# One pair of gate/up units per SwiGLU by block products in place of two, weight loads in written order, the third sum on VectorE, and the SiLU as one ScalarE function

## The chip, the cores and the metric

The kernel runs on one core of a Trainium2 chip, as one program in one launch. The metric is the device time in microseconds from start to end; three runs of the kernel before were timed, and one execution was profiled.

The engines are named as the profile names them: PE is TensorE (its weight loads are shown apart as PEld), DVE is VectorE, ACT is ScalarE, POOL is GpSimd, SP is SyncE, which only issues transfers here. L12 is line 12 of the kernel.

## The reference

Four layers over 256 tokens of width 1024, all in float32. Each layer is: half a SwiGLU, a token mixer beside a cross-attention into 256 memory tokens, and half a SwiGLU again.

```
h = rms_norm(x, ffn_norm[i, 0]);  x = x + 0.5 * swiglu(h, w_gate, w_up, w_down)
h = rms_norm(x, mix_norm[i]);     x = x + concat(mixer(h), memory_attention(h)) @ w_out[i]
h = rms_norm(x, ffn_norm[i, 1]);  x = x + 0.5 * swiglu(h, ...)

swiglu(x, wg, wu, wd) = (silu(x @ wg) * (x @ wu)) @ wd        # 1024 -> 2816 -> 1024
```

The mixer is retention in layers 0 and 3, a sparse attention with an indexer in layer 1, and a three-branch sparse attention in layer 2. The eight SwiGLUs hold most of the work, and the change is in them alone.

## The kernel before

**Tokens and numbers.** The 256 tokens are two blocks of 128, called t = 0 and 1. A float32 number is carried as two parts, `hi` and `lo`: ScalarE rounds a tile to `hi` (a copy), VectorE subtracts to get `lo`. A product is then three TensorE products, hi by hi, hi by lo and lo by hi, each 128x512 out (`mm3`, L292 to L294).

**Units.** Weights come as units of two blocks [128, 2048], 1 MB each. A SwiGLU has eleven gate/up units "g" 0 to 10 (each 256 gate columns and 256 up columns) and six down units "d" 0 to 5, in the order of `FFN_ORDER`: g0 g1 g2 g3 d0 g4 g5 d1 g6 g7 d2 g8 g9 d3 g10 d5 d4. `fetch` issues a unit's loads on SyncE into the tag `raw`, which has three buffers. `split` queues the splitting, in quarters of 128x1024, into the tags `hi` and `lo` with nine buffers each; a tick between the products takes one or two quarters off that queue. A plain unit is 8 products of three for each token block, 48 in all.

**Pairs.** Where a unit's number is in `JOINT`, it and the next are computed together as one joint unit "j", by a block form with seven products in place of eight. The two token blocks by the two halves of the 1024 rows are one 2x2 block matrix, the two units by the same halves (`b11`, `b21`, `b12`, `b22`) are the other. Each of the seven products is 4 x 3 products on TensorE, so a pair takes 84 where two plain units take 96. It needs sums of weight blocks, called `t1` to `t4`, each as two tiles of 128x1024 with the name `sum`:

- `t1` = b12 + b11 and `t3` = b12 + b22 are made by transfers. `start` loads b12 into both on SyncE (L210), `add` has GpSimd issue an adding transfer of the second block (L214).
- `t2` = t1 + b22 and `t4` = t2 + b21 are made by VectorE in place (L233), just ahead of the split into `hi` (L236, ScalarE) and `lo` (L237, VectorE).

The sums have their own buffers (the tag of `t4`, nine of them, shared with the token sums `op`), so they do not wait for a `raw` buffer. The token sums, from `sums`, serve both pairs of a SwiGLU. `joint` writes the seven products with the combinations of their results between them (L484 to L502).

**Order.** The kernel is written in one order, but a planner orders the instructions on each engine's queue, the transfers on SyncE's among them, from the dependences and its own costs. So a transfer that needs no busy buffer can be queued ahead of one written earlier. Waits on buffers are then waits of the issuing queue.

**After a gate/up unit**, `ffn` computes for each token block, with p the product before its row scale r: th = tanh(p_gate * r/2) on ScalarE (L1248), th = (th + 1) * p_gate on VectorE (L1249), h = th * r^2 * p_up on VectorE (L1254). This is twice silu(gate) * up, and 0.25 at the end takes that back. Two units' h are transposed on TensorE (L1262), split again (L1263, L1264), and are what the down units multiply (`acc<-hi,hTh` in the trace). tanh, the attentions' exponentials, Copy and Square all run on ScalarE.

Of the kernel before, what the change touches and what calls it, by code (L numbers as in the profile page):

```python
# [11 lines left out]
AF = mybir.ActivationFunctionType  # L12
OP = mybir.AluOpType
# [9 lines left out]
FFN_ORDER = [("g", 0), ("g", 1), ("g", 2), ("g", 3), ("d", 0), ("g", 4), ("g", 5), ("d", 1),  # L23
             ("g", 6), ("g", 7), ("d", 2), ("g", 8), ("g", 9), ("d", 3), ("g", 10), ("d", 5), ("d", 4)]

JOINT = (4, 8,)


C_CS, C_TRI, C_GI, C_DK, C_CM, C_ANY, C_CCS, C_BM = 0, 256, 384, 390, 396, 524, 525, 653
# [51 lines left out]
class Net:  # L81
    def __init__(self, ctx, tc, a, layers):
        self.tc, self.nc, self.a = tc, tc.nc, a
        self.layers = layers

        def pool(name, **k):
            return ctx.enter_context(tc.tile_pool(name=name, bufs=1, **k))

        self.cp, self.wp, self.ap, self.sp = pool("const"), pool("weights"), pool("act"), pool("small")
        self.ps = pool("psum", space=PSUM)  # L90
        self.units, self.raw, self.parts = [], {}, {}
        self.n_fetch = self.n_split = 0
        self.seq, self.due, self.queue, self.memkv = [], [], [[], []], {}
        self.ticks = 0
        self.jobs, self.open = [], []
        self.extra = []
        self.st, self.splits = [{}, {}], []
        self.plan()
# [30 lines left out]
    def plan(self):  # L129
        a = self.a  # L130

        def ffn(i, j):
            for kind, u in FFN_ORDER:
                if kind == "g" and u in JOINT:
                    self.units.append(("j", [a["gu"][i, j, u, 0], a["gu"][i, j, u, 1], a["gu"][i, j, u + 1, 0],
                                             a["gu"][i, j, u + 1, 1]], None))
                elif kind == "g" and u - 1 in JOINT:
                    continue
# [12 lines left out]
        def both(n):  # L151
            self.seq += [(n, 3)] if self.units[n][0] == "j" else [(n, 0), (n, 1)]

        for j, i in enumerate(self.layers):
# [23 lines left out]
            for u in range(n, len(self.units)):  # L178
                both(u)

    def fetch(self):
        u = self.n_fetch
        if u >= len(self.units):
            return
        self.n_fetch += 1
        if self.units[u][0] == "j":
            self.fetch_joint(u)
            return
        self.raw[u] = []
        for ap in self.units[u][1]:  # L190
            n = ap.shape[1]
            r = self.wp.tile([128, n], F32, name="raw", tag="raw", bufs=3)
            self.nc.sync.dma_start(r, ap)
            self.raw[u].append(r)

    def fetch_joint(self, u):

        nc = self.nc
        b11, b21, b12, b22 = self.units[u][1]
        half = lambda ap, q: ap[:, 1024 * q:1024 * q + 1024]  # L200
        raw = self.raw[u] = {}

        def plain(name, ap):
            raw[name] = self.wp.tile([128, 2048], F32, name="raw", tag="raw", bufs=3)
            nc.sync.dma_start(raw[name], ap)

        def start(name):
            raw[name] = [self.t4([128, 1024], "sum") for _ in range(2)]
            for q in range(2):
                nc.sync.dma_start(raw[name][q], half(b12, q))  # L210

        def add(name, ap):
            for q in range(2):
                nc.gpsimd.dma_start(raw[name][q], half(ap, q), accum_op=OP.add)  # L214

        plain("b11", b11)
        start("t1")
        add("t1", b11)
        plain("b22", b22)
        start("t3")  # L220
        add("t3", b22)
        plain("b21", b21)

    def split_joint(self, u):
        nc = self.nc
        raw, parts = self.raw.pop(u), self.parts[u]
        parts.update({n: [] for n in ("b11", "t1", "t2", "t3", "b21", "t4", "b22")})
        half = lambda n, q: raw[n][:, 1024 * q:1024 * q + 1024] if n[0] == "b" else raw[n][q]

        def quarter(name, src, q, plus):  # L230
            x = half(src, q)
            if plus:
                nc.vector.tensor_add(x, x, half(plus, q))  # L233
            hi = self.wp.tile([128, 1024], F32R, name="hi", tag="hi", bufs=HALVES)
            lo = self.wp.tile([128, 1024], F32R, name="lo", tag="lo", bufs=HALVES)
            nc.scalar.activation(hi, x, AF.Copy)  # L236
            nc.vector.tensor_sub(lo, x, hi.bitcast(F32))  # L237
            parts[name].append((hi, lo))

        for name, src, plus in (("b11", "b11", None), ("t1", "t1", None), ("t2", "t1", "b22"), ("t3", "t3", None),  # L240
                                ("b21", "b21", None), ("t4", "t1", "b21"), ("b22", "b22", None)):
            for q in range(2):
                self.splits.append((u, lambda name=name, src=src, q=q, plus=plus: quarter(name, src, q, plus)))
# [983 lines left out]
    def ffn(self, t, g, st):  # L1227

        nc = self.nc
        H, acc, nd = {}, None, 0  # L1230
        X = self.X[t]
        for kind, ui in FFN_ORDER:
            u = yield
            if not H:
                s, r, rh, r2 = st["n"]
            if kind == "g":
                r_, rh_, r2_ = r, rh, r2
                if u == 0:
                    p = self.first[t]
                elif isinstance(u, tuple):  # L1240
                    p, (_, r_, rh_, r2_) = u
                else:
                    p = self.pB("pg")
                    self.project(p, s, u)
                if t and ui == 0:
                    self.sums()
                th = self.t1([128, 256], "th")
                nc.scalar.activation(th, p[:, :256], AF.Tanh, scale=rh_)  # L1248
                nc.vector.scalar_tensor_tensor(th, th, 1.0, p[:, :256], op0=OP.add, op1=OP.mult)  # L1249

                if ui % 2 == 0:
                    h = self.t2([128, 512], "h")
                hs = h[:, ui % 2 * 256:ui % 2 * 256 + 256]
                nc.vector.scalar_tensor_tensor(hs, th, r2_, p[:, 256:], op0=OP.mult, op1=OP.mult)  # L1254
                if ui % 2 or ui == 10:
                    n = 4 if ui % 2 else 2
                    hl = H[ui // 2] = [self.t2([128, 4, 128], f"hT{x}", F32R) for x in "hl"]

                    def turn(h=h, hl=hl, n=n):
                        c = self.pC("pT")  # L1260
                        for k in range(n):
                            nc.tensor.transpose(c[:, k], h[:, k * 128:k * 128 + 128], self.ident)  # L1262
                        nc.scalar.activation(hl[0][:, :n], c[:, :n], AF.Copy)  # L1263
                        nc.vector.tensor_sub(hl[1][:, :n], c[:, :n], hl[0][:, :n].bitcast(F32))  # L1264

                    self.later(WAIT["h"], turn)
            else:
                pr = self.parts[u]
                if acc is None:
                    acc = self.pA("acc")  # L1270
                nk = len(pr)
                for cb in range(2):
                    for k in range(nk):
                        hl = H[ui]
                        wh, wl = pr[k]
                        o = cb * 512
                        self.mm3(acc[cb], hl[0][:, k], hl[1][:, k], wh[:, o:o + 512], wl[:, o:o + 512],
                                 nd == 0 and k == 0, nd == 5 and k == nk - 1)
                    if nd == 5:
                        xs = X[:, cb * 512:cb * 512 + 512]  # L1280
                        nc.vector.scalar_tensor_tensor(xs, acc[cb], 0.25, xs, op0=OP.mult, op1=OP.add)
                        if g is None:
                            nc.scalar.dma_start(self.a["out"][t * 128:(t + 1) * 128, cb * 512:cb * 512 + 512], xs)
                        else:
                            (self.norm_half if g >= 8 else self.norm_kept)(t, g, cb, st)
                    if cb == 0:
                        self.tick()
                nd += 1
        if g is not None:
            self.norm_stats(t, st)  # L1290
# [303 lines left out]
```

## Time and profile before

| | |
|---|---|
| median of three runs | 2109.27 us (2106.8 to 2116.53) |
| the profiled execution, its own time | 2109.68 us |
| span of its trace, first to last instruction | 2107.9 us |
| TensorE busy, products issued | 2028.5 us, 9486 |
| VectorE, ScalarE, GpSimd busy | 1520.9, 1114.2, 227.7 us |
| mean granted clock of TensorE | 0.985 of full |
| moved by DMA | 402.11 MB, mean 191 GB/s |

Busy time of TensorE is modelled from pipelined products: each is shown as longer than the distance to the next one's start, so the pace is read from starts. The share of the granted clock is that of full speed.

The eight SwiGLUs are a first one up to 200 us, three joined twos from 349 to 718, 860 to 1230 and 1424 to 1795 us, and a last one from 1917 us; mixers lie between.

### The profile page before, as it was taken

Reading aid. Unit: us, or ns where it says so; the run is one execution under the profiler, and the core shown is the slowest. Engines: PE = TensorE matmul, PEld = TensorE weight load, DVE = VectorE, ACT = ScalarE, POOL = GpSimd, SP = SyncE. Lnnn points to the kernel's source line nnn. Section 1 sums busy time; section 2 is a strip of 40 time slices with the busy share of each in tenths; the row PEclk is TensorE's granted clock in tenths of the full one; section 3 lists DMA queues with packets and bytes.
Section 4 is the critical chain, followed back from the end, with each engine's and each line's share of the span. In section 5 each row is a group of like instructions: output and inputs, shape, how many; then the busy total and the mean of one; then the engine's idle time right before and its main releaser. Section 6 shows DMA issues by size and latency. Waiting matters only on the chain.

```text
span 2107.9 us, 25369 instructions
## 1 busy us (share of the span) xinstructions
PE 2028.5 (96%) x9486; PEld 1628.5 (77%) x9486; DVE 1520.9 (72%) x2209; ACT 1114.2 (53%) x1562; POOL 227.7 (11%) x349
## 2 busy tenths in 40 slices
PE   8899999899989999989998999999899989999899
PEld 6677777778867887868777788877788778778687
DVE  7677757778767787867777876667786868658675
ACT  6455655446545555545545554544555545545453
POOL 0100411100100022100000112210000100301000
PEclk9999999999999999999999999999999999999999
DMA  7855535865683533684577443137744774436843
GB/s 260 261 189 220 180 120 200 241 218 200 213 245 143 205 110 120 234 246 145 218 235 242 182 173 130 64 121 235 241 179 180 231 248 181 159 120 215 249 149 126
DMA packets 66988, 402.11 MB, mean 191 GB/s; under 512 B 7600, under 2 KB 8016, under 8 KB 28080
## 3 DMA queue, kind: packets, MB, share of 16 engines
q1 hardware_dynamic: 56304, 364.54, 47.2%
q0 software_dynamic: 9408, 33.97, 8.3%
q10 hardware_dynamic: 1152, 1.97, 0.3%
q8 instruction: 75, 1.23, 0.2%
q14 instruction: 49, 0.40, 0.1%
HBM read 399.40 MB, written 1.05 MB: 190 GB/s over the span
## 4 chain that ended last, share of the span: by engine, by line
PE 74%; DMA 12%; DVE 8%; ACT 3%; issue 2%; POOL 1%; SPq 0%; ACTq 0%; DVEq 0%; POOLq 0%
PE pg L292 8%; PE pg L294 8%; PE pg L293 8%; PE acc L293 7%; PE acc L294 6%; PE acc L292 6%; DMA sum<-gu 5%; DVE lo L237 4%; DMA raw<-gu 3%; PE p L292 3%; DMA raw<-dn 3%; PE p L293 3%; PE p L294 3%; DVE lo L265 2%; PE pT L1262 2%
## 5 line engine op out<-in xcount | busy, mean ns | idle before, releaser
L265 DVE TENSOR_TENSOR lo<-raw,hi 128x1024 fp32r<-128x1024 f32 (+3 forms) x516 | 615.6, 1217 | 175.1 <-ACT hi L264 168.5
L264 ACT ACTIVATE hi<-raw 128x1024 fp32r<-128x1024 f32 (+3 forms) x516 | 527.1, 1046 | 273.0 <-DMA raw<-gu 79.0
L292 PE MATMUL pg<-hi,sh 128*128 128x512 f32 x896 | 354.8, 396 | 4.4 <-ACT hi L1347 3.4
L293 PE MATMUL pg<-lo,sh 128*128 128x512 f32 x896 | 350.7, 391 | 0.7 <-DVE lo L1348 0.7
L294 PE MATMUL pg<-hi,sl 128*128 128x512 f32 x896 | 349.8, 390 | 0.0
L292 PE MATMUL acc<-hi,hTh 128*128 128x512 f32 x704 | 286.0, 410 | 34.9 <-ACT hi L264 34.9
L293 PE MATMUL acc<-lo,hTh 128*128 128x512 f32 x704 | 288.0, 413 | 4.6 <-DVE lo L265 4.4
L294 PE MATMUL acc<-hi,hTl 128*128 128x512 f32 x704 | 282.4, 405 | 0.0
L236 ACT ACTIVATE hi<-sum 128x1024 fp32r<-128x1024 f32 x128 | 132.3, 1057 | 165.4 <-PE acc L294 88.9
L237 DVE TENSOR_TENSOR lo<-sum,hi 128x1024 fp32r<-128x1024 f32 x128 | 154.2, 1226 | 77.6 <-ACT hi L236 75.9
L292 PEld LDWEIGHTS pg<-hi,sh 128*128 128x128 f32 x896 | 168.3, 188 | 39.2 <-ACT hi L1347 4.3
L293 PEld LDWEIGHTS pg<-lo,sh 128*128 128x128 f32 x896 | 168.5, 188 | 35.4 <-DVE lo L1348 2.5
L294 PEld LDWEIGHTS pg<-hi,sl 128*128 128x128 f32 x896 | 168.2, 188 | 35.6 <-DVE sl L1370 0.4
L292 PEld LDWEIGHTS acc<-hi,hTh 128*128 128x128 f32 x704 | 135.8, 193 | 68.6 <-ACT hi L264 38.4
L293 PEld LDWEIGHTS acc<-lo,hTh 128*128 128x128 f32 x704 | 136.0, 193 | 42.0 <-DVE lo L265 14.2
L294 PEld LDWEIGHTS acc<-hi,hTl 128*128 128x128 f32 x704 | 136.4, 194 | 27.9 <-DVE hTl L1264 0.2
L1248 ACT ACTIVATE th<-pg,rh 128x256 f32<-128x256 f32 x128 | 60.3, 471 | 179.4 <-PE pg L294 174.0
L1249 DVE SCALAR_TENSOR_TENSOR th<-th,pg 128x256 f32<-128x256 f32 x128 | 53.5, 418 | 107.6 <-ACT th L1248 107.1
L237 DVE TENSOR_TENSOR lo<-raw,hi 128x1024 fp32r<-128x1024 f32 x96 | 114.9, 1226 | 18.9 <-ACT hi L236 18.9
L292 PE MATMUL p<-hi,sh 128*128 128x512 f32 (+4 forms) x320 | 125.2, 391 | 0.3 <-DVE dq_b L529 0.3
L294 PE MATMUL p<-hi,sl 128*128 128x512 f32 (+4 forms) x320 | 121.2, 379 | 0.0
L293 PE MATMUL p<-lo,sh 128*128 128x512 f32 (+4 forms) x320 | 120.9, 378 | 0.0
(344 smaller groups left out, 3185.0 us busy)
## 6 DMA issues: line engine op xcount, KB each, us to landing
raw<-gu SPq DMA_DIRECT2D x158, 1024.0 KB, 5.0
raw<-dn SPq DMA_DIRECT2D x88, 1024.0 KB, 4.9
sum<-gu SPq DMA_DIRECT2D x64, 512.0 KB, 7.6
sum<-gu POOLq DMA_DIRECT2D x64, 512.0 KB, 11.5
raw<-ret SPq DMA_DIRECT2D x20, 1024.0 KB, 4.8
raw<-wout SPq DMA_DIRECT2D x16, 1024.0 KB, 4.8
raw<-mkv SPq DMA_DIRECT2D x8, 1024.0 KB, 4.8
raw<-nsa SPq DMA_DIRECT2D x6, 1024.0 KB, 4.9
```

What stands on the lines that cost most here:

```text
L236: nc.scalar.activation(hi, x, AF.Copy)
L237: nc.vector.tensor_sub(lo, x, hi.bitcast(F32))
L264: nc.scalar.activation(hi, src, AF.Copy)
L265: nc.vector.tensor_sub(lo, src, hi.bitcast(F32))
L292: mm(out, ah, bh, start=start, stop=False)
L293: mm(out, ah, bl, start=False, stop=False)
L294: mm(out, al, bh, start=False, stop=stop)
L1248: nc.scalar.activation(th, p[:, :256], AF.Tanh, scale=rh_)
L1249: nc.vector.scalar_tensor_tensor(th, th, 1.0, p[:, :256], op0=OP.add, op1=OP.mult)
L1262: nc.tensor.transpose(c[:, k], h[:, k * 128:k * 128 + 128], self.ident)
```

## The change

`JOINT` loses its 8: g8 and g9 become plain units, g4 and g5 stay a pair. Weight loads (`raw` and the sums' first loads) go through a new `load`, which ties each to the one written before it, so that SyncE issues them in written order. In a pair, `t1` is fetched ahead of `b11`, and `t3` is no longer made by transfers: VectorE makes it as t2 - b11 at the time of its split, in a tile of its own. In `ffn`, ScalarE's SiLU takes the place of the tanh and of the first VectorE step, and the factors r^2 and 0.25 become r and 0.5.

```diff
--- before.py
+++ after.py
@@ -23,7 +23,7 @@
 FFN_ORDER = [("g", 0), ("g", 1), ("g", 2), ("g", 3), ("d", 0), ("g", 4), ("g", 5), ("d", 1),
              ("g", 6), ("g", 7), ("d", 2), ("g", 8), ("g", 9), ("d", 3), ("g", 10), ("d", 5), ("d", 4)]
 
-JOINT = (4, 8,)
+JOINT = (4,)
 
 
 C_CS, C_TRI, C_GI, C_DK, C_CM, C_ANY, C_CCS, C_BM = 0, 256, 384, 390, 396, 524, 525, 653
@@ -92,6 +92,7 @@
         self.n_fetch = self.n_split = 0
         self.seq, self.due, self.queue, self.memkv = [], [], [[], []], {}
         self.ticks = 0
+        self.last = self.loaded = None
         self.jobs, self.open = [], []
         self.extra = []
         self.st, self.splits = [{}, {}], []
@@ -178,6 +179,20 @@
             for u in range(n, len(self.units)):
                 both(u)
 
+    def load(self, dst, src):
+
+        self.nc.sync.dma_start(dst, src)
+        i = self.nc.cur_bb.bb.instructions[-1]
+        if self.loaded is not None:
+            self.behind(i, self.loaded)
+        self.loaded = i
+
+    def behind(self, i, j):
+
+        self.tc.add_manual_dep(
+            i, j.name, mybir.DependencyInfo(mybir.DependencyClass.NoSync, mybir.DependencyReason.DATA),
+            reason="in order")
+
     def fetch(self):
         u = self.n_fetch
         if u >= len(self.units):
@@ -190,7 +205,7 @@
         for ap in self.units[u][1]:
             n = ap.shape[1]
             r = self.wp.tile([128, n], F32, name="raw", tag="raw", bufs=3)
-            self.nc.sync.dma_start(r, ap)
+            self.load(r, ap)
             self.raw[u].append(r)
 
     def fetch_joint(self, u):
@@ -202,23 +217,21 @@
 
         def plain(name, ap):
             raw[name] = self.wp.tile([128, 2048], F32, name="raw", tag="raw", bufs=3)
-            nc.sync.dma_start(raw[name], ap)
+            self.load(raw[name], ap)
 
         def start(name):
             raw[name] = [self.t4([128, 1024], "sum") for _ in range(2)]
             for q in range(2):
-                nc.sync.dma_start(raw[name][q], half(b12, q))
+                self.load(raw[name][q], half(b12, q))
 
         def add(name, ap):
             for q in range(2):
                 nc.gpsimd.dma_start(raw[name][q], half(ap, q), accum_op=OP.add)
 
-        plain("b11", b11)
         start("t1")
         add("t1", b11)
+        plain("b11", b11)
         plain("b22", b22)
-        start("t3")
-        add("t3", b22)
         plain("b21", b21)
 
     def split_joint(self, u):
@@ -229,7 +242,11 @@
 
         def quarter(name, src, q, plus):
             x = half(src, q)
-            if plus:
+            if name == "t3":
+                raw.setdefault("t3", []).append(self.t4([128, 1024], "sum"))
+                nc.vector.tensor_sub(raw["t3"][q], x, half("b11", q))
+                x = raw["t3"][q]
+            elif plus:
                 nc.vector.tensor_add(x, x, half(plus, q))
             hi = self.wp.tile([128, 1024], F32R, name="hi", tag="hi", bufs=HALVES)
             lo = self.wp.tile([128, 1024], F32R, name="lo", tag="lo", bufs=HALVES)
@@ -237,7 +254,7 @@
             nc.vector.tensor_sub(lo, x, hi.bitcast(F32))
             parts[name].append((hi, lo))
 
-        for name, src, plus in (("b11", "b11", None), ("t1", "t1", None), ("t2", "t1", "b22"), ("t3", "t3", None),
+        for name, src, plus in (("b11", "b11", None), ("t1", "t1", None), ("t2", "t1", "b22"), ("t3", "t1", None),
                                 ("b21", "b21", None), ("t4", "t1", "b21"), ("b22", "b22", None)):
             for q in range(2):
                 self.splits.append((u, lambda name=name, src=src, q=q, plus=plus: quarter(name, src, q, plus)))
@@ -1245,13 +1262,12 @@
                 if t and ui == 0:
                     self.sums()
                 th = self.t1([128, 256], "th")
-                nc.scalar.activation(th, p[:, :256], AF.Tanh, scale=rh_)
-                nc.vector.scalar_tensor_tensor(th, th, 1.0, p[:, :256], op0=OP.add, op1=OP.mult)
+                nc.scalar.activation(th, p[:, :256], AF.Silu, scale=r_)
 
                 if ui % 2 == 0:
                     h = self.t2([128, 512], "h")
                 hs = h[:, ui % 2 * 256:ui % 2 * 256 + 256]
-                nc.vector.scalar_tensor_tensor(hs, th, r2_, p[:, 256:], op0=OP.mult, op1=OP.mult)
+                nc.vector.scalar_tensor_tensor(hs, th, r_, p[:, 256:], op0=OP.mult, op1=OP.mult)
                 if ui % 2 or ui == 10:
                     n = 4 if ui % 2 else 2
                     hl = H[ui // 2] = [self.t2([128, 4, 128], f"hT{x}", F32R) for x in "hl"]
@@ -1278,7 +1294,7 @@
                                  nd == 0 and k == 0, nd == 5 and k == nk - 1)
                     if nd == 5:
                         xs = X[:, cb * 512:cb * 512 + 512]
-                        nc.vector.scalar_tensor_tensor(xs, acc[cb], 0.25, xs, op0=OP.mult, op1=OP.add)
+                        nc.vector.scalar_tensor_tensor(xs, acc[cb], 0.5, xs, op0=OP.mult, op1=OP.add)
                         if g is None:
                             nc.scalar.dma_start(self.a["out"][t * 128:(t + 1) * 128, cb * 512:cb * 512 + 512], xs)
                         else:
```

## Rows read from the trace of the kernel before

**Rows 1.** The page's first part: busy time of each engine, its share of the span, and its instructions.
```profile
PE 2028.5 (96%) x9486; PEld 1628.5 (77%) x9486; DVE 1520.9 (72%) x2209; ACT 1114.2 (53%) x1562; POOL 227.7 (11%) x349
```

**Rows 2.** Who waited for whom, TensorE alone, longest first: microseconds in total, times, the longest.
```profile
PE acc L292 <- ACT hi L264: 34.9, 8, 5.7
PE pT L1262 <- DVE h L1254: 20.7, 15, 5.1
PE acc L293 <- DVE lo L265: 4.4, 12, 0.5
```

**Rows 3.** TensorE in order of time, around two waits of down products (start, duration, engine, line, what; idle time before it and what ended it).
```profile
96.78 0.73 PE L292 MATMUL acc<-hi,hTh 128*128 128x512 f32 x2 [0.77 <-ACT hi L264]
...
401.88 0.39 PE L474 MATMUL pg<-hi,sh 128*128 128x512 f32 x1
...
415.34 0.39 PE L476 MATMUL pg<-hi,sl 128*128 128x512 f32 x1
...
416.73 0.40 PE L294 MATMUL acc<-hi,hTl 128*128 128x512 f32 x1
422.15 0.80 PE L292 MATMUL acc<-hi,hTh 128*128 128x512 f32 x1 [5.03 <-ACT hi L264]
423.41 0.80 PE L293 MATMUL acc<-lo,hTh 128*128 128x512 f32 x1 [0.46 <-DVE lo L265]
...
428.62 0.39 PE L475 MATMUL pg<-lo,op 128*128 128x512 f32 x1
```

**Rows 4.** Two stretches of 20 us, around the down block that follows the pair at unit 4 and around the one that follows the pair at unit 8 of the same SwiGLU: busy time of each engine (instructions), the granted clock, the DMA's share and GB/s.
```profile
412.00:432.00 20.00, 14.51 (x51) 11.08 (x50) 11.22 (x13) 7.62 (x9) 1.75 (x2) 0.83 1.04 324
486.00:506.00 20.00, 20.00 (x91) 15.79 (x91) 18.43 (x24) 12.06 (x16) 0.00 (x0) 1.00 0.78 297
```

**Rows 5.** ScalarE in order of time, after the pair at unit 4.
```profile
412.16 1.99 ACT L264 ACTIVATE hi<-raw 128x1024 fp32r<-128x1024 f32 x2
421.04 2.00 ACT L264 ACTIVATE hi<-raw 128x1024 fp32r<-128x1024 f32 x2 [6.89 <-DMA raw<-dn]
```

**Rows 6.** SyncE's queue in order of time around the same pair (start, and time until the last of the group was issued).
```profile
387.07 0.33 SPq L193 DMA_DIRECT2D raw<-dn  x1
403.53 4.87 SPq L210 DMA_DIRECT2D sum<-gu  x3
409.20 0.33 SPq L193 DMA_DIRECT2D raw<-dn  x1
411.64 0.33 SPq L210 DMA_DIRECT2D sum<-gu  x1
```

**Rows 7.** The loads issued by line L193: time to landing of the one issued at 409.20, then the one issued at 483.6 (duration of the issue, first and last start) and its time to landing.
```profile
DMA to landing us min/median/max: 11.7/11.7/11.7
...
L193 SPq DMA_DIRECT2D raw<-dn x1: 327/327/327, 483.6 to 483.6; - x1
DMA to landing us min/median/max: 4.6/4.6/4.6
```

**Rows 8.** The page's list of transfers: KB each, median time from issue to landing.
```profile
raw<-dn SPq DMA_DIRECT2D x88, 1024.0 KB, 4.9
```

**Rows 9.** TensorE and ScalarE in order of time at the pair at unit 8: the pair's first product, the splits of its down block, and two products of that block.
```profile
476.21 0.39 PE L474 MATMUL pg<-hi,sh 128*128 128x512 f32 x1
...
486.48 3.89 ACT L264 ACTIVATE hi<-raw 128x1024 fp32r<-128x1024 f32 x4
...
491.32 0.40 PE L292 MATMUL acc<-hi,hTh 128*128 128x512 f32 x1
491.67 0.49 PE L293 MATMUL acc<-lo,hTh 128*128 128x512 f32 x1
```

**Rows 10.** Instructions grouped by line: count, busy microseconds, mean nanoseconds of one, idle time before them.
```profile
L488 DVE TENSOR_TENSOR s<-pg,s 128x512 f32<-128x512 f32 x16 | 11.0, 686 | 0.0
...
L1249 DVE SCALAR_TENSOR_TENSOR th<-th,pg 128x256 f32<-128x256 f32 x128 | 53.5, 418 | 107.6 <-ACT th L1248 107.1
```

**Rows 11.** One stretch of plain units (columns as in rows 4).
```profile
442.00:464.00 22.00, 22.00 (x101) 18.19 (x100) 14.19 (x17) 11.15 (x14) 0.00 (x0) 1.00 0.52 196
```

**Rows 12.** VectorE in order of time during the pair at unit 4.
```profile
401.14 3.50 DVE L237 TENSOR_TENSOR lo<-sum,hi 128x1024 fp32r<-128x1024 f32 x3 [3.69 <-ACT hi L236]
...
407.95 1.22 DVE L233 TENSOR_TENSOR sum<-sum,raw 128x1024 f32<-128x1024 f32 x1
...
411.53 2.35 DVE L237 TENSOR_TENSOR lo<-raw,hi 128x1024 fp32r<-128x1024 f32 x2
413.80 2.35 DVE L265 TENSOR_TENSOR lo<-raw,hi 128x1024 fp32r<-128x1024 f32 x2
```

**Rows 13.** ScalarE and TensorE in order of time at the start of a pair: in the SwiGLU of rows 3, and in the first one.
```profile
390.05 1.06 ACT L236 ACTIVATE hi<-sum 128x1024 fp32r<-128x1024 f32 x1 [2.42 <-DMA sum<-gu]
...
69.27 0.78 PE L292 MATMUL acc<-hi,hTh 128*128 128x512 f32 x1
...
73.26 0.52 PE L292 MATMUL acc<-hi,hTh 128*128 128x512 f32 x1
```

**Rows 14.** ScalarE's table loads by line; then the sums over windows: the attentions' exponential (L584) over the five SwiGLU stretches, and the SwiGLU's tanh (L1248) over the four mixers.
```profile
L1377 ACT ACT_TABLE_LOAD x1 | 1.3, 1283 | 6.2 <-DMA gains<-gains 6.2
...
sum 1477.00, ACT 0.00; mean ACT 0.00
sum 590.00, ACT 0.00; mean ACT 0.00
```

## The prediction

> **What bounds the kernel now.** I read the page's busy shares first, then who waited for whom on TensorE, then the order of time around the longest of those waits.
>
> TensorE is busy for 96% of the span [rows 1]. A faster VectorE or ScalarE is therefore worth only what it takes out of TensorE's waits, while TensorE's own work counts in full. The waits are few: 34.9 us in 8 waits of down-projection products on the upper half (`hi`) of a weight, and 20.7 us in 15 waits of transposes on `h` [rows 2].
>
> Seven of the eight are one event, once in each SwiGLU but the first. Take the one at 417 us. TensorE issues a product every 0.228 us (from 401.88 to 415.34, 59 steps), stops in the down block that follows the pair at unit 4 in the code (written "d",1; d1 here), and stays idle for 5.03 us and again for 0.46 us. It comes back slow: the 13 starts from 422.15 to 428.62 are 0.50 apart [rows 3]. The granted clock of that stretch is 0.83, a mixture of the two levels of 2.4 and 1.2 GHz [rows 4]. From the start at 416.73 to that at 428.62 lie 14 products; at 0.228 each they would take 3.2 us and took 11.9. So **one such stop costs 8.7 us**, of which 3.2 is slow clock. The mean wait of the seven is a little shorter ((34.9 - 0.77) / 7 = 4.9 against 5.03; the 0.77 is the eighth, in the first SwiGLU [rows 3]), so I count 8.5.
>
> What ends it is a load. ScalarE splits d1's first block at 412.16 and then idles for 6.89 us until the second is there [rows 5]. SyncE issues that second block at 409.20, and it needs 11.7 us to land [rows 6, 7]; the median of such a block is 4.9 us [rows 8]. Ahead of it in the queue stand three half-block loads, issued from 403.53, and one follows at 411.64 [rows 6]: the sums of the *other* pair, at unit 8, whose products begin at 476.21 [rows 9]. They and their adds hold the DMA at a share of 1.04 [rows 4].
>
> The pair at unit 8 is the control. Its down block's second load was issued 7.4 us after the pair's first product (483.6 against 476.21), as d1's was (409.2 against 401.88), with no sum beside it. It landed in 4.6 us [rows 7]. ScalarE split all four quarters in one run, and TensorE lost about 0.1 us (0.35 between two starts in place of 0.23) [rows 9].
>
> **The change part by part.**
>
> *Pair at unit 8 becomes two plain units.* A pair is 7 x 4 x 3 = 84 products, two plain units are 2 x 2 x 8 x 3 = 96. So 8 x 12 x 0.228 = **+21.9 us** of TensorE [rows 3], all of it on the path. Off the path VectorE loses, in each SwiGLU, 6 splits and 4 sums of 1.22 us [rows 12] and 5 combinations of 0.69 [rows 10]: 15.6 us, 125 us in all. That is worth nothing in itself: in a plain stretch VectorE is busy for 14.2 of 22 us [rows 11].
>
> *Its half-block transfers go too*, four loads and four adds in each SwiGLU, and with them what delayed d1. With the median landing, d1's second block is there at 409.2 + 4.9 = 414.1 and its first quarter is split at 415.2; TensorE asks for it at 416.96. So seven stops go: 7 x 8.5 = **-59.5 us**. I leave 0.5 us in each SwiGLU, between the control's 0.1 and 0.7: VectorE's splits of the two quarters, if they run on behind those that end at 416.2 [rows 12], end at 418.6, and the product that reads the last is due four starts after 416.96, at 417.9. That is **+4 us**.
>
> *Third sum on VectorE.* Two subtractions of 1.22 us for each remaining pair, 19.5 us in all. They can run as soon as the second sums stand, where VectorE idles for 3.69 us before 401.14 [rows 12]: nothing. Without that gap they would push d1's splits back by up to 2.4 us; that lies inside the range. In exchange `b11` is held longer. Its buffer went to d1's first block at 387.07 [rows 6]; now it goes free only after the third sum, by 401 in that gap, or 409 at worst, since the fourth sum, which overwrites the same tile, began at 407.95 [rows 12]. At 401 the block is there by 406 and is split at 412 as before.
>
> *Loads in written order, first sum first.* The only loads that I find far ahead of their turn are unit 8's sums, which vanish; so the order by itself I put at nothing. Putting `t1` ahead of `b11`, with two half loads and two adds less beside it, matters at the pair's start. There ScalarE waits 2.42 us for the sum to land, the SiLU's tanh stands behind it, then two VectorE steps, then TensorE's transpose. In the first SwiGLU TensorE comes back from such a wait at half rate (9 steps from 69.27 to 73.26, 4.0 us in place of 2.05: 2 us lost) [rows 13].
>
> *SiLU in one step.* ScalarE's instruction keeps its shape; VectorE loses 176 x 0.42 = 74 us [rows 10]. Off the path, except that the chain to the transpose is 0.4 us shorter. With the part above, of the 20.7 us in 15 waits [rows 2] I take 12, and the 2 us of slow clock: **-14 us**. The bounds are nothing and all 22.7.
>
> ScalarE must however fetch another table. One load of 1.28 us serves the whole run now; no exponential runs in the SwiGLU stretches and no SwiGLU tanh outside them [rows 14]. With Copy and Square in both sets it is one load at each crossing, 9 x 1.28 = 12 us of an engine 53% busy [rows 1], hidden by the units that TensorE has ready. Fully exposed it is +12.
>
> The Trainium skill ("ScalarE: Activation LUTs", What ACT_TABLE_LOAD costs) puts a switch at some 2.66 us, load and drain together; the trace's load agrees (1283 ns), the drain is not seen here. By that, nine exposed switches would be 24 us.
>
> **Sum.** Against the profiled execution's own 2109.68 us (span 2107.9; the median of three runs is 2109.27, so no correction): 2109.7 + 21.9 - 59.5 + 4 - 14 = **2062 us**, 2.2% faster.
>
> **Rivals.**
>
> *A. Stops shortened, not gone.* d1's second block might get `b22`'s buffer in place of `b21`'s. `b22`'s last split ends at 413.9 [rows 12]; plus 4.9 and 1.05 that is 419.9, a wait of 2.9 + 0.46 and perhaps 1.9 of slow clock: 5.3 in place of 8.5. Then 7 x 3.2 = 22 us are won in place of 55.5: **2095**. For it: which buffer it is hangs on a planner's order that will be made anew. Against it: the order of the splits (second sum, fourth, `b22` itself) is unchanged.
>
> *B. Stops unchanged.* The late block is not the sums' doing, or another load takes their place: 2062 + 55.5 = **2117**, or 2131 if the transposes' waits stay as well. Against it stands the control, with the same issue time.
>
> *C. The other side: the tables.* If the set with the SiLU lacked the Copy that ScalarE runs between SiLUs, each SiLU would cost two loads: 2 x 176 x 1.28 = 451 us. In a plain stretch ScalarE would rise from 11.2 of 22 us [rows 11] by four SiLUs x 2.56 to 21.4, and beyond 22 at the pair, where it has six more splits. It decides from the point where ScalarE needs TensorE's whole 22 us; I put some 8 us for each SwiGLU on B's case: **about 2180**. One load that serves Copy, Square, tanh and exponential together [rows 14] speaks against it. The same page of the Trainium skill (Table sets) says that copy is in every set as filler; no run here shows it for this set.
>
> *D. The order as a cost.* SyncE, bound to written order, could hold `b11` behind a `t1` that waits for its tile, and d1 with it. It would look like A, and I count it there.
>
> **How the numbers follow.** Stops gone 0.72, A 0.12, B 0.11, C 0.05. The forecast's own range runs from all waits gone and no residue (2109.7 + 21.9 - 60.9 - 22.7 - 4 for the waits on the lower halves, 2044) to exposed tables and none of the transposes' waits won (2062 + 14 + 12 = 2088). To leave out no more than 2 in 10 the range reaches to A: 2042 to 2096. A measurement of this kernel tells 0.5% (10.5 us) from no change. Forecast and A are faster: 0.84. B is mostly within: 0.09. The rest of B, and C, slower: 0.07.
>
> **What would show it.** Right: in the seven SwiGLUs no wait over 2 us of `acc` on `hi`, a granted clock near 1.0 there, d1's second load landing in about 5 us, 9582 TensorE products, the new plain units' at 0.228 us, and about nine table loads. Wrong: `acc` still waiting 4 us or more behind a load that lands late; more than some thirty table loads; or new waits on VectorE's third sum. The forecast hangs above all on d1's second block being issued before about 411.

## The result

The changed kernel takes 2045.03 us in the median of four runs (2042.98 to 2045.96), where the kernel before, in the same session, takes 2109.91: a ratio of 0.9691, 95% interval 0.9671 to 0.971. That is 3.1% faster. The forecast was 2062 us (2042 to 2096): right in its sign, its mechanism and its range, and 17 us too slow.

The profiled execution took 2042.98 us. Its page, first the span, then the engines' busy time and instructions; then who waited for whom on TensorE, of which these are the lines that answer to [rows 2]:

```profile
span 2041.2 us, 24905 instructions
PE 2019.7 (99%) x9582; PEld 1637.8 (80%) x9582; DVE 1365.5 (67%) x1929; ACT 1081.0 (53%) x1515; POOL 182.2 (9%) x301
```

```profile
PE pT L1278 <- DVE h L1270: 1.9, 1, 1.9
...
PE acc L310 <- DVE lo L282: 0.3, 2, 0.2
```

TensorE does 96 products more, as counted, and is idle for 2041.2 - 2019.7 = 21.5 us in place of 79.4. The waits of down products on `hi` have no line any more (34.9 us in [rows 2]), those of transposes on `h` are down from 20.7 us to one of 1.9. VectorE lost 155 us of work; nothing shows that this was worth anything in itself.

The same place as in [rows 3], the second SwiGLU: TensorE in order of time from the pair's first product across what was the stop, then VectorE, SyncE and ScalarE around it.

```profile
391.83 0.40 PE L491 MATMUL pg<-hi,sh 128*128 128x512 f32 x1
...
405.53 0.39 PE L309 MATMUL acc<-hi,hTh 128*128 128x512 f32 x1
...
406.69 0.40 PE L311 MATMUL acc<-hi,hTl 128*128 128x512 f32 x1
406.93 0.40 PE L309 MATMUL acc<-hi,hTh 128*128 128x512 f32 x1
407.29 0.50 PE L310 MATMUL acc<-lo,hTh 128*128 128x512 f32 x1
407.63 0.39 PE L311 MATMUL acc<-hi,hTl 128*128 128x512 f32 x1
...
409.25 0.39 PE L491 MATMUL pg<-hi,op 128*128 128x512 f32 x1
```

```profile
385.70 2.36 DVE L247 TENSOR_TENSOR sum<-sum,raw 128x1024 f32<-128x1024 f32 x2
...
388.12 11.39 SPq L184 DMA_DIRECT2D raw<-dn  x2
...
391.09 3.49 DVE L254 TENSOR_TENSOR lo<-sum,hi 128x1024 fp32r<-128x1024 f32 x3 [1.90 <-ACT hi L253]
...
402.11 3.89 ACT L281 ACTIVATE hi<-raw 128x1024 fp32r<-128x1024 f32 x4
```

d1's first fifteen products run from 405.53 to the pair's next one at 409.25 without a stop; two starts 0.36 and 0.34 us behind the one before are the whole trace of it, where 5.42 lay between 416.73 and 422.15 before. ScalarE splits all four quarters in one run of 3.89 us: it no longer waits for the second block. That block is the second of the two loads of SyncE's line, issued at 399.2. These are its issue and its time to landing, then the granted clock, DMA share and GB/s of the 20 us around (they answer to [rows 7] and [rows 4]):

```profile
L184 SPq DMA_DIRECT2D raw<-dn x1: 328/328/328, 399.2 to 399.2; - x1
...
DMA to landing us min/median/max: 4.7/4.7/4.7
```

```profile
402.00:422.00 20.00, 20.00 (x91) 15.80 (x90) 17.40 (x21) 12.33 (x17) 0.00 (x0) 1.00 0.75 285
```

4.7 us in place of 11.7, at the full clock. The third sums (L247) run at 385.7, in the stretch where VectorE had idled; of the 3.69 us of [rows 12] 1.90 are left.

ScalarE's table loads by line: five for the SiLU, four for the exponential, one at the start.

```profile
L1265 ACT ACT_TABLE_LOAD x5 | 6.4, 1283 | 6.1 <-PE pg L311 6.0
L601 ACT ACT_TABLE_LOAD x4 | 5.1, 1283 | 4.7 <-DVE nb L598 4.7
...
L1393 ACT ACT_TABLE_LOAD x1 | 1.3, 1283 | 5.9 <-DMA gains<-gains 5.9
```

### The profile page after: what moved, and what is told of

Its sections match the earlier page's. It is cut to its first block, busy times and chain, and to the rows that moved or that the text cites. A ratio compares the mean times of both kernels' runs of the same rounds, so it can differ in the third digit from the quotient of the medians.

```text
span 2041.2 us, 24905 instructions
## 1 busy us (share of the span) xinstructions
PE 2019.7 (99%) x9582; PEld 1637.8 (80%) x9582; DVE 1365.5 (67%) x1929; ACT 1081.0 (53%) x1515; POOL 182.2 (9%) x301
## 4 chain that ended last, share of the span: by engine, by line
PE 91%; DVE 4%; DMA 2%; ACT 2%; issue 1%; POOL 1%; SPq 0%; ACTq 0%; DVEq 0%
PE pg L309 12%; PE pg L311 12%; PE pg L310 12%; PE acc L310 8%; PE acc L309 8%; PE acc L311 8%; PE p L309 3%; PE p L310 3%; PE p L311 3%; PE pT L1278 2%; PE pg L492 1%; PE pg L491 1%; PE pg L493 1%; PE pT L564 1%; PE po L309 1%; PE po L310 1%
## 5 line engine op out<-in xcount | busy, mean ns | idle before, releaser
L282 DVE TENSOR_TENSOR lo<-raw,hi 128x1024 fp32r<-128x1024 f32 (+1 forms) x580 | 692.9, 1218 | 255.5 <-ACT hi L281 240.9
L281 ACT ACTIVATE hi<-raw 128x1024 fp32r<-128x1024 f32 (+1 forms) x580 | 594.1, 1047 | 290.8 <-PE acc L311 124.6
L309 PE MATMUL pg<-hi,sh 128*128 128x512 f32 x1152 | 455.1, 395 | 4.2 <-ACT hi L1363 3.1
L310 PE MATMUL pg<-lo,sh 128*128 128x512 f32 x1152 | 449.8, 390 | 0.7 <-DVE lo L1364 0.7
L311 PE MATMUL pg<-hi,sl 128*128 128x512 f32 x1152 | 450.3, 391 | 0.0
L309 PEld LDWEIGHTS pg<-hi,sh 128*128 128x128 f32 x1152 | 216.7, 188 | 48.6 <-ACT hi L1363 4.0
L1265 ACT ACTIVATE th<-pg,rstd 128x256 f32<-128x256 f32 x152 | 72.0, 474 | 243.9 <-PE pg L311 243.7
L1270 DVE SCALAR_TENSOR_TENSOR h<-th,rstd,pg 128x256 f32<-128x256 f32 x152 | 72.5, 477 | 160.8 <-ACT th L1265 160.8
L253 ACT ACTIVATE hi<-sum 128x1024 fp32r<-128x1024 f32 x64 | 66.1, 1057 | 80.1 <-PE acc L311 44.5
L254 DVE TENSOR_TENSOR lo<-sum,hi 128x1024 fp32r<-128x1024 f32 x64 | 76.7, 1229 | 20.8 <-ACT hi L253 19.8
```

The costliest lines, as they stand in the source:

```text
L281: nc.scalar.activation(hi, src, AF.Copy)
L282: nc.vector.tensor_sub(lo, src, hi.bitcast(F32))
L309: mm(out, ah, bh, start=start, stop=False)
L310: mm(out, ah, bl, start=False, stop=False)
L311: mm(out, al, bh, start=False, stop=stop)
L1265: nc.scalar.activation(th, p[:, :256], AF.Silu, scale=r_)
```

## The experiments

The theory was: each stop is a collision of d1's second load with the sums of the *other* pair, which a queue without order lets overtake it. One rival was that the pairs' work on VectorE and ScalarE made the stops, so that one pair had to go; another, for the waits of transposes, was the length of the SiLU's chain. Times are medians beside runs of the kernel before on the same chip (2107.8 to 2110.7 us).

| run | pairs | order tied | t1 written ahead of b11 | third sum | SiLU | us | ratio, 95% interval |
|---|---|---|---|---|---|---|---|
| before | 2 | no | no | transfers | tanh | 2109.9 | 1 |
| e1_one_pair_only | 1 | no | no | transfers | tanh | 2057.5 | 0.9757 [0.9722, 0.9792] |
| e3_order_only | 2 | yes | no | transfers | tanh | 2088.6 | 0.990 [0.987, 0.993] |
| e9_order_t1_first | 2 | yes | yes | transfers | tanh | 2030.7 | 0.9617 [0.9593, 0.9641] |
| e7_two_pairs_t3_dma | 2 | yes | yes | transfers | SiLU | 2028.7 | 0.9611 [0.9584, 0.9638] |
| e10_two_pairs_b11_first | 2 | yes | no | VectorE | SiLU | 2037.6 | 0.9649 [0.9629, 0.967] |
| e2_two_pairs_new | 2 | yes | yes | VectorE | SiLU | 2027.6 | 0.9628 [0.9584, 0.9672] |
| e6_two_pairs_no_order | 2 | no | yes | VectorE | SiLU | 2073.5 | 0.9824 [0.9792, 0.9857] |
| e5_no_order | 1 | no | yes | VectorE | SiLU | 2045.8 | 0.9696 [0.9674, 0.9717] |
| e4_tanh_back | 1 | yes | yes | VectorE | tanh | 2048.3 | 0.9718 [0.9683, 0.9753] |
| changed kernel | 1 | yes | yes | VectorE | SiLU | 2045.0 | 0.9691 [0.9671, 0.971] |
| e8_three_pairs | 3 | yes | yes | VectorE | SiLU | 2150.5 | 1.0196 [1.017, 1.0221] |

### One pair, nothing else: e1_one_pair_only

```diff
-JOINT = (4, 8,)
+JOINT = (4,)
```

> The kernel before with the pair at unit 8 turned into two plain units and nothing else. If the late load of d1 was the collision with the other pair's sums, all seven stops of 8.5 us go and 21.9 us of products come: some waits of transposes stay (10 to 15 us), so 2070 to 2078 us, and d1's second block lands in about 5 us. If the stops came from VectorE's and ScalarE's load at the pair, or from the order of the weight loads, they stay here in part: 2090 us or more.

2057.5 us. The stops go without any other edit: TensorE's waits have no line of `acc` on `hi`, and d1's second load, issued at 407.0, lands in 4.8 us. First its waits, then that load.

```profile
PE pT L1262 <- DVE h L1254: 14.0, 8, 5.0
...
PE acc L293 <- DVE lo L265: 0.7, 4, 0.2
```

```profile
L193 SPq DMA_DIRECT2D raw<-dn x1: 328/328/328, 407.0 to 407.0; - x1
...
DMA to landing us min/median/max: 4.8/4.8/4.8
```

The waits of transposes stay at 14.0 us, as expected. The time is still 13 us under the range that I gave: 6.7 us of such waits (20.7 to 14.0) went with the second pair.

### Order, nothing else: e3_order_only

```diff
+    def load(self, dst, src):
+        self.nc.sync.dma_start(dst, src)
+        i = self.nc.cur_bb.bb.instructions[-1]
+        if self.loaded is not None:
+            self.behind(i, self.loaded)
+        self.loaded = i
...
-            self.nc.sync.dma_start(r, ap)
+            self.load(r, ap)
-            nc.sync.dma_start(raw[name], ap)
+            self.load(raw[name], ap)
-                nc.sync.dma_start(raw[name][q], half(b12, q))
+                self.load(raw[name][q], half(b12, q))
```

> The kernel before with the weight loads and the sums' first loads tied in written order and nothing else (two pairs, third sum by transfers, b11 first, tanh). Collision theory: the seven stops go with no products added, 2109.9 - 59.5 = 2050, plus up to 15 us of waits at the second pair, whose sums now come as late as the first one's: 2050 to 2065 us. Rival, the amount transferred and split: no change, 2105 us or more.

2088.6 us: both ranges missed. The trace says why. All waits of `acc` on `hi` are gone, as the collision theory has it, and a new wait has taken their place: transposes on `h`, 47.1 us in place of 20.7.

```profile
PE pT L1277 <- DVE h L1269: 47.1, 10, 9.5
```

ScalarE and TensorE in order of time at the second pair, and the landing of the add that is waited for (issued at 449.7):

```profile
464.50 1.06 ACT L251 ACTIVATE hi<-sum 128x1024 fp32r<-128x1024 f32 x1 [4.38 <-DMA sum<-gu]
465.46 0.46 ACT L1263 ACTIVATE th<-pg,rh 128x256 f32<-128x256 f32 x1
...
467.95 0.69 PE L1277 MATMUL pT<-ident,h 128*128 128x128 f32 x2 [4.72 <-DVE h L1269]
468.29 0.78 PE L308 MATMUL acc<-lo,hTh 128*128 128x512 f32 x1
```

```profile
L229 POOL DMA_DIRECT2D sum<-gu x1: 876/876/876, 449.7 to 449.7; - x1
...
DMA to landing us min/median/max: 14.7/14.7/14.7
```

Tied to their turn, the second pair's sums are issued when `b11`, `b22` and `b21` are, and share the DMA with them. ScalarE's queue is in order: its split of the late sum stands ahead of the tanh, the tanh ahead of `h`, `h` ahead of the transpose. Overtaking had one use: it made those sums early.

### Order and t1 first: e9_order_t1_first

```diff
-        plain("b11", b11)
         start("t1")
         add("t1", b11)
+        plain("b11", b11)
```

> As e3_order_only (2088.6 us), with one thing more: t1's loads and adds are written ahead of b11's. Two pairs, third sum by transfers, tanh. In e3 the second half of t1 landed 14.7 us after its add was issued, ScalarE waited 4.4 us for it and the tanh stood behind. If the place of t1 is what costs there, the waits at the second pair shrink to under 1.5 us: 2028 to 2045 us. If the amount of transfers (third sum) or the longer tanh chain is what costs, most of it stays: 2065 us or more.

2030.7 us. One line moved saves some 58 us more. The transposes' waits fall to 5.9 us in 2, and ScalarE waits 1.12 us for the sum where it waited 4.38:

```profile
PE pT L1277 <- DVE h L1269: 5.9, 2, 5.6
```

```profile
448.12 1.06 ACT L251 ACTIVATE hi<-sum 128x1024 fp32r<-128x1024 f32 x1 [1.12 <-DMA sum<-gu]
449.09 0.45 ACT L1263 ACTIVATE th<-pg,rh 128x256 f32<-128x256 f32 x1
```

VectorE's work is that of the kernel before, 1518.6 us against 1520.9, and no wait of `acc` on `hi` is left. That rules out its load as the cause of the stops.

### Both pairs with all the rest: e2_two_pairs_new, and what each of the rest is worth

```diff
-JOINT = (4,)
+JOINT = (4, 8,)
```

> The changed kernel with both pairs (4 and 8) kept; order, third sum on VectorE and SiLU as changed. If the collision is what costs, the written order alone keeps the second pair's sums behind d1, and the second pair gives its 12 products back: 2045 - 21.9 = 2023, plus 0 to 15 us of new waits, 2023 to 2038 us. If giving up the second pair was what made the kernel faster, the stops come back: 2075 us or more.

2027.6 us, 17 less than the changed kernel, within the range for the collision theory. The pair at unit 8 was worth keeping: its 12 products in each SwiGLU come back and no stop does.

e7_two_pairs_t3_dma makes the third sum by transfers in e2's place.

```diff
         plain("b22", b22)
+        start("t3")
+        add("t3", b22)
         plain("b21", b21)
...
-            if name == "t3":
-                raw.setdefault("t3", []).append(self.t4([128, 1024], "sum"))
-                nc.vector.tensor_sub(raw["t3"][q], x, half("b11", q))
-                x = raw["t3"][q]
-            elif plus:
+            if plus:
...
-        for name, src, plus in (..., ("t3", "t1", None),
+        for name, src, plus in (..., ("t3", "t3", None),
```

> As e2_two_pairs_new, with the third sum made by transfers again (two half loads and two adds for each pair, in written order after b22). e3_order_only lost 4 to 6 us at each second pair, where ScalarE waited for a sum. Theory: those sums are late because four loads and four adds share the DMA with b11, b22 and b21; with t1 first the first sum is early but the third is not, so part of it stays: 2040 to 2070 us. Rival, the place of t1 ahead of b11 is all that matters: 2025 to 2033 us.

2028.7 us, no difference that can be told: here the rival was right. With `t1` first, the transfers of the third sum do no harm that the time shows.

e10_two_pairs_b11_first has the third sum on VectorE and puts `b11` ahead of `t1` again.

```diff
-        start("t1")
-        add("t1", b11)
         plain("b11", b11)
+        start("t1")
+        add("t1", b11)
```

> As e2_two_pairs_new (2027.6 us), with b11's load written ahead of t1's again; third sum on VectorE, SiLU. If the place of t1 is what matters, waits of transposes come back at the pairs, 1 to 5 us each in sixteen pairs: 2040 to 2075 us. If fewer transfers are enough whatever the order of the two, 2026 to 2033 us.

2037.6 us, between the two ranges. It has five waits of transposes, but one of 8.0 us in the first SwiGLU is nearly all of them:

```profile
PE pT L1278 <- DVE h L1270: 9.4, 5, 8.0
```

So in the later SwiGLUs either remedy is enough, `t1` first or the third sum off the DMA (the second only as far as tried: e10 has the SiLU besides, and no run has it with the tanh). In the first, `t1` must come first: e2 has 1.6 us there and e9, with the tanh, 5.6.

### The order taken away: e6_two_pairs_no_order and e5_no_order

Both have this edit, e6 with two pairs and e5 with one:

```diff
-        if self.loaded is not None:
-            self.behind(i, self.loaded)
```

> As e2_two_pairs_new (2027.6 us), without the tie of the loads to written order. Collision theory: unit 8's first sums overtake d1's second load again, now with half the transfers (two half loads and two adds in place of four and four), so the stops come back in part, 2 to 6 us each in seven SwiGLUs: 2040 to 2085 us. Rival, halving the sums' transfers is enough by itself: 2025 to 2033 us.

2073.5 us: 46 more than with the order. The stops are back, shorter. TensorE's waits; SyncE's queue and TensorE at d1, in order of time; the landing of its second load (issued at 405.23); and the granted clock, DMA share and GB/s of 20 us around the stop:

```profile
PE acc L307 <- ACT hi L279: 21.3, 8, 3.7
PE acc L308 <- DVE lo L280: 6.1, 10, 0.8
```

```profile
399.51 1.46 SPq L184 DMA_DIRECT2D sum<-gu  x2
405.23 0.33 SPq L184 DMA_DIRECT2D raw<-dn  x1
...
415.42 0.51 PE L307 MATMUL acc<-hi,hTh 128*128 128x512 f32 x1 [2.26 <-ACT hi L279]
416.68 0.79 PE L308 MATMUL acc<-lo,hTh 128*128 128x512 f32 x1 [0.75 <-DVE lo L280]
```

```profile
DMA to landing us min/median/max: 9.0/9.0/9.0
```

```profile
412.00:432.00 20.00, 16.99 (x71) 12.99 (x70) 13.53 (x18) 9.94 (x13) 0.00 (x0) 0.91 0.82 297
```

This is the collision with half the sums, two half loads and two adds where the kernel before has four and four. These are GpSimd's issues of the adds, in e6 and then in the kernel before:

```profile
404.18 0.87 POOL L227 DMA_DIRECT2D sum<-gu  x1 [28.10 <-DVE lo L252]
406.16 0.86 POOL L227 DMA_DIRECT2D sum<-gu  x1 [1.11 <-DVE s L503]
```

```profile
408.01 0.86 POOL L214 DMA_DIRECT2D sum<-gu  x1 [26.59 <-DMA sum<-gu]
410.18 0.87 POOL L214 DMA_DIRECT2D sum<-gu  x1 [1.30 <-DVE s L488]
416.39 0.87 POOL L214 DMA_DIRECT2D sum<-gu  x1 [5.33 <-DVE lo L265]
```

Not all of them stand beside d1's load. In e6 both half loads have landed by 405.6, so its company until 414.2 is the two adds and, from 409.90, the next unit's loads. In the kernel before, from 409.20 to 420.9, it is three adds, two half loads (issued at 408.1 and 411.6; a third lands at 409.7) and, from 413.91, the next unit's loads. With none of them d1's second load lands in 4.7 us, here in 9.0 and 11.7 ([rows 7]); TensorE waits 0, 2.3 and 5.0 us. So in e6 the delay begins beside the adds of the overtaking sums, not beside their first loads; no run takes the two apart for the kernel before.

> The changed kernel without the tie of the loads to written order (one pair, t1 first, third sum on VectorE, SiLU stay). Theory: with one pair there is no second pair's sum to overtake anything, so the order is worth nothing here: 2042 to 2050 us. Rival, the order is what keeps d1's load early: stops of TensorE on acc come back, 2060 us or more.

2045.8 us, no difference from the changed kernel. No sum stands ahead of d1's loads. The edit undoes more than it names: SyncE's queue has one of the pair's plain blocks ahead of `t1`'s loads again, in every SwiGLU but the first (e6's first pairs too).

```profile
360.29 0.33 SPq L184 DMA_DIRECT2D raw<-gu  x1
360.67 0.90 SPq L184 DMA_DIRECT2D sum<-gu  x2
```

So with one pair and the third sum on VectorE, neither the order nor the place of `t1` in the later SwiGLUs is worth anything that can be told: transposes wait 3.3 us in all here.

### The SiLU: e4_tanh_back

```diff
-                nc.scalar.activation(th, p[:, :256], AF.Silu, scale=r_)
+                nc.scalar.activation(th, p[:, :256], AF.Tanh, scale=rh_)
+                nc.vector.scalar_tensor_tensor(th, th, 1.0, p[:, :256], op0=OP.add, op1=OP.mult)
...
-                nc.vector.scalar_tensor_tensor(hs, th, r_, p[:, 256:], op0=OP.mult, op1=OP.mult)
+                nc.vector.scalar_tensor_tensor(hs, th, r2_, p[:, 256:], op0=OP.mult, op1=OP.mult)
...
-                        nc.vector.scalar_tensor_tensor(xs, acc[cb], 0.5, xs, op0=OP.mult, op1=OP.add)
+                        nc.vector.scalar_tensor_tensor(xs, acc[cb], 0.25, xs, op0=OP.mult, op1=OP.add)
```

> The changed kernel with tanh and its VectorE step in place of the SiLU (no other edit undone). Theory: VectorE is off the path, the step costs only where a transpose waits for h: 2045 to 2050 us, with one table load in place of ten. Rival, that the shorter chain is what took the 19 us of transposes' waits: 2055 us or more.

2048.3 us: 3.3 more, less than the two intervals can tell from nothing. The trace shows where it may come from: one wait of 5.1 us in the first SwiGLU is back (1.9 with the SiLU); the later ones have none. VectorE is busy for 65 us more and nothing waits for it.

### Three pairs: e8_three_pairs

```diff
-             ("g", 4), ("g", 5), ("d", 1), ("g", 6), ("g", 7), ("d", 2), ("g", 8), ...
+             ("g", 4), ("g", 5), ("g", 6), ("d", 1), ("g", 7), ("d", 2), ("g", 8), ...
-JOINT = (4,)
+JOINT = (2, 5, 8)
```

> The changed kernel with three pairs, at units 2, 5 and 8 (the SwiGLU's order is g0 g1 j2 d0 g4 j5 d1 g7 d2 j8 d3 g10 d5 d4). Each pair takes 12 products out of each SwiGLU, 21.9 us in all, and brings VectorE about 18 us in each; VectorE was busy for 74% with two pairs. If TensorE's products stay the bound: 2006 to 2015 us. If VectorE becomes the bound at the pairs, or the token sums are not ready for a pair as early as unit 2: new waits, 2028 us or more.

2150.5 us, slower than the kernel before. TensorE issues 96 products less than there and waits longer: its waits, the page's busy line of this kernel, and its core's granted clock.

```profile
PE pg L491 <- ACT s L501: 31.8, 8, 9.1
PE pg L491 <- ACT op L454: 16.8, 8, 2.3
```

```profile
PE 2031.7 (95%) x9390; PEld 1619.0 (75%) x9390; DVE 1623.1 (76%) x2201; ACT 1182.5 (55%) x1627; POOL 209.6 (10%) x333
```

```profile
core 0: 2147.6 us, clock 0.975
```

The eight and eight are the first pair of each SwiGLU. Its products wait for token sums (`op`) and for the copy `s` that stands behind them and behind weight splits on ScalarE: at unit 2 the token sums are still being made. VectorE's mean of 76% shows none of this. Two more groups add 32.8 us (`pg` on `h` 16.6 in 12, `pR` on `rb`, a step of the token sums, 16.2 in 4). In all TensorE is idle for 2147.6 - 2031.7 = 115.9 us, 36.5 more than before, and a mean clock of 0.975 lacks 53.7 us of the span where 0.985 lacked 31.6: 22 us more. How three pairs would do at later units was not tried.

### The two beside each other: e11_two_pairs_again and e12_changed_again

> e2_two_pairs_new again, beside the changed kernel on the same chip, to have the two apart by more than their noise: 2024 to 2031 us.

> The changed kernel again, unchanged: 2043 to 2048 us, some 17 us (0.8%) above e11_two_pairs_again.

2026.5 and 2044.7 us on one chip; to the kernel before 0.960 [0.9579, 0.962] and 0.9686 [0.9665, 0.9706]. The version with two pairs is the fastest one here, by 0.9% over the changed kernel.

## Why the prediction was right, and where it was off

**The stops.** Right as a mechanism: seven of them, ended by one load, delayed by the other pair's sums. The control (the same load at the same moment of the second pair) had said so, and e1, e3 and e6 show it from three sides. Rivals A and B did not happen: d1's second load was issued 7.4 us after the pair's first product, as before, and landed in 4.7. The prediction named the half loads ahead in the queue first and their adds after them; by the landing times the adds weigh more: the first of the three half loads had landed at 407.4, before d1's load was issued, and in e6 the adds stand beside it almost alone when the delay begins.

**The 21.9 us of products.** Near. The plain units in the place of the second pair run at 0.227 us (84 starts from 457.24 to 476.05). With the pair kept, e2 is 17.5 us and e11 18.2 us under the changed kernel, for the same 96 products: it has small waits of its own (TensorE idle for 24.3 against 21.5 us in e2, 24.7 against 23.8 in e11 and e12), and the other 1.6 and 2.8 us I can't assign.

**The sum.** Between the two profiled executions lie 2109.7 - 2043.0 = 66.7 us, where the sum had 47.6. TensorE's idle time fell by 57.9 us; the sum had 37.3 of it in the seven stops (7 x (4.87 + 0.46)) and 12 in the transposes, less the 4 of residue: 45.3. So 12.6 us were mis-sized there. The transposes' waits were worth 18.8 us, not 12. The residue was 0.3 us of idle time, not 4 (by starts 0.24 us at the place shown, 0.70 for the two steps from 406.93 to 407.63, where the sum had 0.5). The rest is the eighth stop and smaller waits of lower halves, most of them in the first SwiGLU. The slow clock was sized well: a mean of 0.985 over 2107.9 us lacks 31.6 us, one of 0.997 over 2041.2 lacks 6.1, so 25.5 came back where the sum had 24.4. That leaves 88.6 - 57.9 - 25.5 = 5.2 us, where 88.6 is 66.7 + 21.9. They are about what the idle time leaves out: a wait counts from the modelled end of the product before it, 0.39 us after its start, where the next could have started after 0.228. Of the 35 waits in [rows 2] 3 are left, and 32 x 0.16 = 5.1 us, an estimate. In e1, reckoned in the same way, 3.5 us are left, and 23 waits fewer make 3.7.

**Where the 17 us lie.** e1 splits the change. The pair by itself is worth 2107.75 - 2057.53 = 50.2 us beside its own runs of the kernel before, where the sum had 59.5 - 21.9 - 4 = 33.6 for it. The other parts, from e1 to the changed kernel, give 12.5, where it had 14. So the term that was mis-sized is the pair's. 6.7 us of the transposes' waits left with it, which the sum expected from `t1` and the SiLU; the eighth stop (0.77) and part of the residue are smaller items, and no run takes the rest apart.

**"The order by itself I put at nothing."** Right for the changed kernel (e5: 0.8 us, within noise), and the wrong question. I saw that the overtaking loads were the second pair's and concluded that they vanish with it. I did not ask what the order would do with the pair kept. There it is worth 46 us (e6 against e2), and the pair's 12 products need not be given up.

**The third sum and the place of t1.** That VectorE's idle stretch takes the sums: right, at 385.7. That `b11`'s buffer is held longer and nothing waits: right (d1's first block was issued at 388.12 and split at 402.11). What the prediction priced together as 14 us was not pulled apart by it. Of the transposes' waits 3.2 us are the SiLU's, in the first SwiGLU alone (5.1 in e4, 1.9 in the changed kernel), and 8.9 belong to the order, `t1` and the third sum together (14.0 in e1, 5.1 in e4).

**The tables.** Ten loads of 1283 ns, one more than the nine crossings for the start. So rival C is out: Copy and Square run between the SiLUs without a load. TensorE's waits did not grow behind the loads: on the exponential's output they are 1.7 us in 2 where they were 2.0 in 2, and e4, with one load, is not faster. The "some 2.66 us" of the Trainium skill ("ScalarE: Activation LUTs", What ACT_TABLE_LOAD costs) could not show in the time either way; its load agrees with the trace, its drain no line here shows. After the load at 729.92 ScalarE's next instruction starts at 731.22, 1.30 us later.

## What to carry to other kernels

When a wait ends on a load, look at what the queue issued ahead of it and for when that is needed: here transfers for work 60 us away delayed the one due in 8. The twin of a slow place in the same trace, with one thing different, tells more than any busy share. And before giving up the user of a resource to end a collision, try to move its transfers: ordering them and starting the first needed one earlier gave some 80 us (e9), where dropping the user gave some 50 (e1).

## What the runs showed of the hardware that was not expected

One 1 MB load takes 4.7 us to land by itself, 9.0 with two half-block adds from GpSimd beside it (and the next unit's loads from halfway), and 11.7 with three adds, two half-block loads and the next unit's loads. I had expected a delay, not that two adds nearly double the time. And a short stop costs more than its idle time: around 2.26 and 0.75 us of idling in e6, the granted clock of 20 us is 0.91, a mixture of 2.4 and 1.2 GHz, where the changed kernel, without a stop, has 1.00 in the same place.
